# Attention values as rows of tokens: four heads to a job, the weights as the moving side

## The chip, the cores and the metric

The kernel runs on one core of one Trainium2 chip. The metric is the time of one execution on the device in microseconds (us). The kernel before takes 3025.03 us, the median of three runs (3024.79, 3025.03 and 3029.89).

## What is computed

Two transformer blocks follow each other on 256 tokens of width 2048. The change lies in the first one, in its mixer. One projection of the normed input gives queries, keys and values of two attentions of eight heads each, width 128 a head. The first is stick-breaking attention, the second a softmax over keys that an indexer picks; only the second's queries and keys go through rope.

```
proj = h @ w_in
q_a, k_a, v_a, q_b, k_b, v_b, qi, ki, wi, g_a, g_b = split(proj)
y_a = stick_breaking_attention(q_a, k_a, v_a) @ w_a          # 8 heads of 128
y_b = dsa_attention(rope(q_b), rope(k_b), v_b, rope(qi), rope(ki), wi) @ w_b
merged = sigmoid(g_a) * y_a + sigmoid(g_b) * y_b
out = merged @ w_o
```

In both attentions the last step is `w @ v`, a sum over tokens, so it needs the values with tokens on the 128 partitions.

## The kernel before

Every matrix product is a list of *jobs* that one loop, `run`, works off in order. A job of the projection covers 128 output columns. Its weights come in one DMA of 1 MB from `w_in` into a tile `raw` (16 K-tiles of 128x128). The job goes in four *slices* of four K-tiles. For each slice ScalarE (ACT) rounds the weights to fp32r (`whi`) and VectorE (DVE) takes the rest (`wlo`); ACT does so six slices ahead of TensorE (PE), DVE five (`LEAD`). The activations `h` were split in the same way before. TensorE then does three matmuls for each K-tile, `whi·h_hi`, `whi·h_lo` and `wlo·h_hi`, with the 128x128 weights as the stationary side and the 256 tokens as the moving side: 12 matmuls a slice, 48 a job. The result stands in a PSUM tile `g` with output columns on the partitions and tokens along the row.

When a job's last slice has been issued, `run` calls its epilogue `epi`, and then `advance`, as it does after each slice. `advance` lets up to three generators of the list `fill` go one step; each `yield n` of a generator puts its next step off by n slices. What a generator issues on TensorE therefore stands between two slices. An engine takes its instructions in the order in which they were written.

The heads' jobs come as q, k, v of the first head, then of the second, and so on: eight heads of the stick-breaking attention, then eight of the other. The epilogues are:

- `cp_epi` (q and k of the first attention): ACT copies `g` into an SBUF tile `a`.
- `rp_epi` (q and k of the second): four DVE operations, `rope`.
- `v_epi` (values of both): ACT copies `g` to `a`; one slice later a generator transposes the two 128x128 halves on TensorE into a PSUM tile `m` (line 800), and ACT copies them to the tile that the attention reads.

With the value job's epilogue the head's own generator, `sb_gen` or `dsa_gen`, is put into `fill`. It yields until its head's values are there, and then issues the product of queries and keys into an `m` tile as its first step. The later steps (softmax, and `pv`, the product with the values) come up to nine slices later. Beside them run the indexer (`index_gen`, from the first value job on) and a background sum for the modulation on DVE (`acc<-ra,csil,acc`).

All matmuls are issued by the helper on line 271, all ACT operations on line 229, DVE's on lines 242, 256 and 262. In the kernel after, these lines stand one further down.

Of the kernel before, what the change touches and what calls it, by code (L numbers as in the profile page):

```python
# [17 lines left out]
D = 2048  # L18
KT = 16
S = 256  # L20
# [103 lines left out]


class Job:
    def __init__(self, chunks, mv, n, epi, pre=None, outs=None, group=None, need=None, gate=False):
        self.chunks = chunks
        self.mv = mv
        self.n = n  # L130
        self.epi = epi
        self.pre = pre
        self.nk = sum(c[1] for c in chunks)
        self.outs = outs or [(0, self.nk)]
        self.group = group
        self.need = need
        self.gate = gate


class Builder:  # L140
# [258 lines left out]
    def run(self, jobs):  # L399
        order = []  # L400
        i = 0
        while i < len(jobs):
# [5 lines left out]
            for j in grp:  # L408
                sl, k = [], 0
                for ci, (_, nk) in enumerate(j.chunks):  # L410
                    for o in range(0, nk, 4):
                        n = min(4, nk - o)
# [7 lines left out]
        chunks = []  # L420
# [100 lines left out]
        for i, (j, ci, o, k, n) in enumerate(order):  # L521
            if j.gate:
                if (i - gi) % 4 == 0:
                    gated(i)
                continue
            if j.group == "h1":
                j.need(k + n)
                pump_dma()
            if self.lazy:
                pump_hi(i + LEAD)  # L530
                pump_lo(i + LOMIN)
                for x in range(LOMIN + 1, LEAD):
                    if self.backlog() < QW:
                        pump_lo(i + x)
            else:
                pump_lo(i + LEAD - 1)
                pump_hi(i + LEAD)
                pump_lo(i + 1)
            if id(j) not in ps:
                if j.pre is not None:  # L540
                    j.pre()
                ps[id(j)] = [self.pg.tile([128, 512], F32, name="g", tag="g") for _ in j.outs]
            if j.need is not None:
                j.need(min(j.nk, k + n + 4))
            hi, lo = wt.pop(i)
            for q in range(n):
                kk = k + q
                oi = next(x for x, (a0, n0) in enumerate(j.outs) if a0 <= kk < a0 + n0)
                a0, n0 = j.outs[oi]
                out = ps[id(j)][oi][:, :j.n]  # L550
                mh, ml = j.mv(kk)
                self.mm(out, hi[:, q], mh, start=(kk == a0), stop=False)
                self.mm(out, hi[:, q], ml, start=False, stop=False)
                self.mm(out, lo[:, q], mh, start=False, stop=(kk == a0 + n0 - 1))
            if k + n == j.nk:
                j.epi(*ps.pop(id(j)))
            self.advance()
# [230 lines left out]
        self.busy = False  # L788
        yield

    def v_epi(self, store, h):
        def epi(ps):
            t = self.a()
            self.act(t[:, :S], ps[:, :S])

            def g():
                yield
                p = self.mps()
                for k in range(2):
                    self.nc.tensor.transpose(p[:, 128 * k:128 * k + 128], t[:, 128 * k:128 * k + 128], self.ident)  # L800
                o = self.a()
                self.act(o[:, :S], p[:, :S])
                store[h] = o
                yield
            self.later(g())
        return epi

    def sb_gen(self, h):
        scale = 128.0 ** -0.5
        while h not in self.va:  # L810
            yield
        q, k, v = self.qa.pop(h), self.ka.pop(h), self.va.pop(h)
        zp = self.mps()
        self.mm(zp[:, 0:256], k[:, 0:128], q[:, 0:256])
        self.mm(zp[:, 256:384], k[:, 128:256], q[:, 128:256])
        zs = self.sc()
        self.act(zs, zp[:, :384], scale=scale)
        e = self.sc()
        self.act(e, zs, AF.Abs)
        yield 2  # L820
        self.act(e, e, AF.Exp, scale=-1.0)
        self.act(e, e, AF.Ln, bias=1.0)
        sp = self.sc()
        self.stt(sp, zs, 0.0, e, ALU.max, ALU.add)
        past, npast = self.cmm("past"), self.cmm("npast")
        for o in (0, 256):
            self.mul(sp[:, o:o + 128], sp[:, o:o + 128], past)
            self.add(zs[:, o:o + 128], zs[:, o:o + 128], npast)
        yield 4
        cp = self.mps()  # L830
        tri = self.cmm("tri")
        self.mm(cp[:, 0:128], tri, sp[:, 0:128])
        self.mm(cp[:, 128:256], tri, sp[:, 128:256], stop=False)
        self.mm(cp[:, 128:256], self.ones, sp[:, 256:384], start=False)
        self.mm(cp[:, 256:384], tri, sp[:, 256:384])
        self.sub(zs, zs, cp[:, :384])
        self.act(zs, zs, AF.Exp)
        yield 3
        self.pv(zs, v, self.ya, h)
        yield  # L840
# [8 lines left out]

    def dsa_gen(self, h):  # L850
        scale = 128.0 ** -0.5
        while h not in self.vb or self.g_idx in self.fill:
            yield
        q, k, v = self.qb.pop(h), self.kb.pop(h), self.vb.pop(h)
        lp = self.mps()
        self.mm(lp[:, 0:128], q[:, 0:128], k[:, 0:128])
        self.mm(lp[:, 128:384], q[:, 128:256], k[:, 0:256])
        L = self.sc()
        self.stt(L, lp[:, :384], scale, self.smask)
        nm, sm, rs = self.tiny(), self.tiny(), self.tiny()  # L860
        segs = ((0, 128), (128, 384))
        for i, (lo, hi) in enumerate(segs):
            self.nc.vector.tensor_reduce(nm[:, i:i + 1], L[:, lo:hi], mybir.AxisListType.X, ALU.max, negate=True)
        yield 2
        for i, (lo, hi) in enumerate(segs):
            self.act(L[:, lo:hi], L[:, lo:hi], AF.Exp, bias=nm[:, i:i + 1], accum_out=sm[:, i:i + 1])
        self.nc.vector.reciprocal(rs[:, 0:2], sm[:, 0:2])
        for i, (lo, hi) in enumerate(segs):
            self.ts(L[:, lo:hi], L[:, lo:hi], rs[:, i:i + 1])
        yield 3  # L870
        pt = self.mps()
        for o in (0, 128, 256):
            self.nc.tensor.transpose(pt[:, o:o + 128], L[:, o:o + 128], self.ident)
        p = self.sc()
        self.act(p, pt[:, :384])
        yield 2
        self.pv(p, v, self.yb, h)
        yield

    def build_mixer(self):  # L880
# [9 lines left out]
        def wj(epi, pre=None, group=None):  # L890
            jobs.append(Job([(ap["w_in"][nb[0]], KT)], mvh, S, epi, pre, group=group, need=lambda k: self.mod1(k)))
            nb[0] += 1
# [12 lines left out]
        def cp_epi(store, hh):  # L905
            def epi(ps):
                t = self.a()
                self.act(t[:, :S], ps[:, :S])
                store[hh] = t
            return epi  # L910

        def rp_epi(store, hh):
            def epi(ps):
                store[hh] = self.rope(ps, self.cosq, self.sinq)
            return epi
# [3 lines left out]
        def with_gen(epi, make, lst):  # L919
            def f(ps):  # L920
                epi(ps)
                lst.append(self.later(make()))
            return f

        for hh in range(NH):
            wj(cp_epi(self.qa, hh), pre=start_idx if hh == 0 else None)
            wj(cp_epi(self.ka, hh))
            wj(with_gen(self.v_epi(self.va, hh), lambda hh=hh: self.sb_gen(hh), sbg))
        for hh in range(NH):
            wj(rp_epi(self.qb, hh))  # L930
            wj(rp_epi(self.kb, hh))
            wj(with_gen(self.v_epi(self.vb, hh), lambda hh=hh: self.dsa_gen(hh), dsg))

        mg = {}
        self.mg = mg
# [1015 lines left out]


_W = {
    "w_in": (89, 128, KT, 128), "w_ada": (D, 6 * D), "w_a": (KT, 128, 8, 128), "w_b": (KT, 128, 8, 128),
    "w_o": (KT, 128, KT, 128), "w_up": (2 * FT, 128, KT, 128), "w_down": (NQ, KT, 128, FQ, 128),
    "w_in_2": (52, 128, KT, 128), "lora": (8, 128, 4, 128), "w_out_2": (KT, 128, KT, 128),
    "w_gu_2": (2 * FT, 128, KT, 128), "w_down_2": (NQ, KT, 128, FQ, 128),
# [3 lines left out]
def _blocks(w, order=None):  # L1961
    k, n = w.shape
    b = w.reshape(k // 128, 128, n // 128, 128).transpose(2, 1, 0, 3)
    if order is not None:
        b = b[order]
    return np.ascontiguousarray(b)
# [15 lines left out]
def layout(inp):  # L1982
# [13 lines left out]
    qi = w[:, o[6]:o[7]].reshape(D, 8, 2, 2, 32).transpose(0, 1, 3, 2, 4).reshape(D, 1024)  # L1996
    cols = [kw, qi]
    for h in range(NH):
        for s in range(3):
            cols.append(w[:, o[s] + 128 * h:o[s] + 128 * h + 128])  # L2000
    for h in range(NH):
        for s in range(3, 6):
            cols.append(w[:, o[s] + 128 * h:o[s] + 128 * h + 128])
    for s in (9, 10):
        for j in range(KT):
            cols.append(w[:, o[s] + 128 * j:o[s] + 128 * j + 128])
    out["w_in"] = _blocks(np.concatenate(cols, 1))
    out["w_ada"] = np.ascontiguousarray(g["w_ada"][0])
    out["w_a"] = _blocks(g["w_a"][0])
    out["w_b"] = _blocks(g["w_b"][0])  # L2010
# [82 lines left out]
```

## Time and profile before

| what | value |
|---|---|
| median of three runs | 3025.03 us |
| the profiled execution's own time | 3029.85 us |
| its span in the profile | 3028.1 us |
| TensorE busy, share of the span | 98% |
| VectorE busy | 72% |
| ScalarE busy | 52% |
| granted TensorE clock, mean | 0.99 |

The profiled execution is one execution, taken by the hardware profiler; its span is what the trace covers, and its own time is 1.75 us more. It lies at the upper end of the three runs. TensorE's busy share is that of a pipeline, in which a matmul's row begins when the one before it is still on its way; the time between two starts tells the pace.

### The profile page before, as it was taken

The page shows a single profiled execution, that of the slowest core. Times are in us where ns is not written, and L with a number is a line of the kernel's source. Part 1 is how long each engine was busy: PE and PEld are TensorE (multiplying, and loading weights), DVE is VectorE, ACT ScalarE, POOL GpSimd, SP SyncE. Part 2 cuts the span into 40 slices and gives each one's busy share as a digit, 9 for nine tenths or more (in the row PEclk, how much of TensorE's full clock was granted, in tenths as well). Part 3 has the DMA queues.
Part 4 walks back from the last instruction along what each step waited for, and adds up shares of the span by engine and source line. Part 5 has one row for each costly group of instructions (what it writes and reads, how often), then busy time and mean ns, then how long its engine had stood idle before and what let it go on. Part 6 is the DMA issues. An engine that isn't in the chain of part 4 may idle for free.

```text
span 3028.1 us, 66212 instructions
## 1 busy us (share of the span) xinstructions
PE 2975.4 (98%) x27088; PEld 2944.3 (97%) x27088; DVE 2185.2 (72%) x4516; ACT 1573.9 (52%) x3214; POOL 161.6 (5%) x295
## 2 busy tenths in 40 slices
PE   7999999999999999999999999999999999999997
PEld 7999999999999999999999999999999999999997
DVE  6787798677887667676677867777577556566565
ACT  1256544444556556565567545444565555454454
POOL 1000000000210000000002000001000000000002
PEclk9799999999999999999999999999999999999998
DMA  9867677787875554555545433233445454554543
GB/s 343 307 219 250 220 261 264 255 288 263 316 261 184 179 190 168 202 181 177 189 163 188 160 116 116 89 108 125 140 151 197 167 198 173 202 181 167 198 162 129
DMA packets 123473, 594.18 MB, mean 196 GB/s; under 512 B 12832, under 2 KB 19360, under 8 KB 81056
## 3 DMA queue, kind: packets, MB, share of 16 engines
q1 hardware_dynamic: 103200, 518.60, 48.9%
q0 software_dynamic: 19968, 71.35, 7.4%
q8 instruction: 212, 3.47, 0.4%
q14 instruction: 93, 0.76, 0.1%
HBM read 585.68 MB, written 4.21 MB: 195 GB/s over the span
## 4 chain that ended last, share of the span: by engine, by line
PE 95%; DVE 3%; DMA 2%; ACT 0%; issue 0%; SPq 0%; POOL 0%; DVEq 0%; ACTq 0%; POOLq 0%
PE g L271 85%; PE m L271 9%; DMA ch<-w_ada 1%; DVE wlo L242 0%; DMA a<-xT 0%; DVE a L262 0%; DVE a L242 0%; PE m L1414 0%; DVE o L242 0%; DMA cm<-cmask 0%; DVE fa L262 0%; DMA raw<-w_up 0%; ACT a L229 0%; DVE acc L262 0%; DVE p L242 0%
## 5 line engine op out<-in xcount | busy, mean ns | idle before, releaser
L271 PE MATMUL g<-a,whi 128*128 128x256 f32 (+2 forms) x11920 | 2187.2, 285 | 2.4 <-ACT a L229 1.9
L271 PEld LDWEIGHTS g<-a,whi 128*128 128x128 f32 x11920 | 1845.7, 189 | 14.1 <-ACT a L229 2.0
L271 PE MATMUL g<-a,wlo 128*128 128x256 f32 (+3 forms) x5960 | 1684.1, 283 | 1.5 <-DVE wlo L242 1.5
L229 ACT ACTIVATE whi<-raw 128x512 fp32r<-128x512 f32 (+1 forms) x1852 | 1093.4, 617 | 519.3 <-PE g L271 495.5
L242 DVE TENSOR_TENSOR wlo<-raw,whi 128x512 fp32r<-128x512 f32 (+1 forms) x1852 | 1212.9, 681 | 132.2 <-ACT whi L229 130.8
L271 PEld LDWEIGHTS g<-a,wlo 128*128 128x128 f32 x5960 | 1127.1, 189 | 2.9 <-DVE wlo L242 2.6
L271 PE MATMUL g<-h,whi 128*128 128x256 f32 x1408 | 248.9, 281 | 0.0
L271 PE MATMUL g<-ex,whi 128*128 128x258 f32 x1232 | 227.1, 284 | 0.0
L271 PEld LDWEIGHTS g<-h,whi 128*128 128x128 f32 x1408 | 214.9, 188 | 0.0
L271 PE MATMUL g<-h,wlo 128*128 128x256 f32 x704 | 197.8, 281 | 0.0
L271 PEld LDWEIGHTS g<-ex,whi 128*128 128x128 f32 x1232 | 191.3, 190 | 0.0
L262 DVE SCALAR_TENSOR_TENSOR acc<-ra,csil,acc 128x512 f32<-128x512 f32 x240 | 182.1, 759 | 3.9 <-DMA ra<-w_ada 3.9
L229 ACT ACTIVATE a<-a 128x256 f32<-128x256 f32 (+5 forms) x303 | 120.9, 410 | 106.4 <-DVE a L242 79.6
L271 PE MATMUL g<-ex,wlo 128*128 128x258 f32 x616 | 174.9, 284 | 0.3 <-DVE wlo L242 0.3
L262 DVE SCALAR_TENSOR_TENSOR a<-a,pc 128x255 f32<-128x255 f32 (+5 forms) x340 | 163.6, 482 | 5.5 <-ACT a L229 0.5
L229 ACT ACTIVATE a<-a,pc 128x256 f32<-128x256 f32 (+2 forms) x214 | 116.8, 547 | 58.6 <-DVE a L242 53.2
L242 DVE TENSOR_TENSOR a<-g,rb 128x258 f32<-128x258 f32 x80 | 34.1, 426 | 154.4 <-PE g L271 154.4
L635 POOL TENSOR_TENSOR a<-a 128x256 f32<-128x256 f32 x59 | 54.1, 927 | 1673.1 <-ACT a L229 1618.2
L229 ACT ACTIVATE a<-g 128x256 f32<-128x256 f32 (+3 forms) x121 | 46.2, 384 | 179.8 <-PE g L271 179.6
L271 PEld LDWEIGHTS g<-h,wlo 128*128 128x128 f32 x704 | 135.2, 192 | 0.0
L271 PE MATMUL m<-p 64*64 64x64 f32 x3328 | 133.6, 219 | 0.1
L262 DVE SCALAR_TENSOR_TENSOR a<-a 128x256 f32<-128x256 f32 (+3 forms) x275 | 116.6, 424 | 11.7 <-ACT a L229 7.7
(171 smaller groups left out, 1848.3 us busy)
## 6 DMA issues: line engine op xcount, KB each, us to landing
raw<-w_in SPq DMA_DIRECT2D x141, 1024.0 KB, 5.8
raw<-w_up SPq DMA_DIRECT2D x88, 1024.0 KB, 4.9
raw<-w_down SPq DMA_DIRECT2D x128, 704.0 KB, 4.1
raw<-w_gu SPq DMA_DIRECT2D x88, 1024.0 KB, 4.9
ra<-w_ada POOLq DMA_DIRECT2D x128, 512.0 KB, 5.4
ch<-w_ada SPq DMA_DIRECT2D x64, 512.0 KB, 7.5
raw<-w_o SPq DMA_DIRECT2D x16, 1024.0 KB, 7.2
raw<-w_out SPq DMA_DIRECT2D x32, 512.0 KB, 3.6
```

Source lines behind the costliest of these rows:

```text
L229: self.nc.scalar.activation(out, in_, f, **kw)
L242: self.nc.vector.tensor_tensor(out, a, b, op)
L262: self.nc.vector.scalar_tensor_tensor(out, a, s, b, op0, op1)
L271: self.nc.tensor.matmul(out, l, r, start=start, stop=stop)
L635: self.nc.gpsimd.tensor_tensor(q[:, :n], q[:, :n], acc[:, :n], ALU.add)
```

## The change

The values are no longer 16 jobs of 128 columns but four *wide* jobs of 512 columns, four heads each. The weights of the values leave `w_in` for an array `w_v`, in which a slice is one K-tile of 512 columns. In a wide job the activations are the stationary side, 128 tokens at a time, and the weights are the moving side, 512 columns: per slice two token halves by three matmuls, each into one of two PSUM tiles. The result has tokens on the partitions, so `v_epi` copies 128x128 pieces, eight ACT operations for four heads, and the transposes and the copies behind them go. A wide job stands ahead of each group of four heads, whose jobs are then q and k alone. The heads' generators are now put into `fill` by the epilogue of k, and wait for k instead of v.

```diff
@@ run
-            for q in range(n):
+            if j.wide:
+                kk, last = k // 4, k + n == j.nk
+                wh, wl = (t.rearrange("p q c -> p (q c)") for t in (hi, lo))
+                mh, ml = j.mv(kk)
+                for t in range(2):
+                    out, c = ps[id(j)][t], slice(128 * t, 128 * t + 128)
+                    self.mm(out, mh[:, c], wh, start=kk == 0, stop=False)
+                    self.mm(out, mh[:, c], wl, start=False, stop=False)
+                    self.mm(out, ml[:, c], wh, start=False, stop=last)
+            for q in range(0 if j.wide else n):
@@ v_epi
-    def v_epi(self, store, h):
-        def epi(ps):
-            t = self.a()
-            self.act(t[:, :S], ps[:, :S])
-
-            def g():
-                yield
-                p = self.mps()
-                for k in range(2):
-                    self.nc.tensor.transpose(p[:, 128 * k:128 * k + 128], t[:, 128 * k:128 * k + 128], self.ident)
-                o = self.a()
-                self.act(o[:, :S], p[:, :S])
-                store[h] = o
-                yield
-            self.later(g())
+    def v_epi(self, store, h0):
+        def epi(*ps):
+            for h in range(4):
+                o = store[h0 + h] = self.a()
+                for t in range(2):
+                    self.act(o[:, 128 * t:128 * t + 128], ps[t][:, 128 * h:128 * h + 128])
         return epi
@@ sb_gen
-        while h not in self.va:
+        while h not in self.ka:
@@ dsa_gen
-        while h not in self.vb or self.g_idx in self.fill:
+        while h not in self.kb or self.g_idx in self.fill:
@@ build_mixer
+        def vj(s, h0, pre=None):
+            w = ap["w_v"][2 * s + h0 // 4]
+            jobs.append(Job([(w[g], KT) for g in range(4)], mvh, S, self.v_epi(self.vb if s else self.va, h0), pre,
+                            outs=[(0, 2 * KT), (2 * KT, 2 * KT)], wide=True))
+
         for hh in range(NH):
-            wj(cp_epi(self.qa, hh), pre=start_idx if hh == 0 else None)
-            wj(cp_epi(self.ka, hh))
-            wj(with_gen(self.v_epi(self.va, hh), lambda hh=hh: self.sb_gen(hh), sbg))
+            if hh % 4 == 0:
+                vj(0, hh, pre=start_idx if hh == 0 else None)
+            wj(cp_epi(self.qa, hh))
+            wj(with_gen(cp_epi(self.ka, hh), lambda hh=hh: self.sb_gen(hh), sbg))
         for hh in range(NH):
+            if hh % 4 == 0:
+                vj(1, hh)
             wj(rp_epi(self.qb, hh))
-            wj(rp_epi(self.kb, hh))
-            wj(with_gen(self.v_epi(self.vb, hh), lambda hh=hh: self.dsa_gen(hh), dsg))
+            wj(with_gen(rp_epi(self.kb, hh), lambda hh=hh: self.dsa_gen(hh), dsg))
```

**Where the product of queries and keys stands on TensorE, stick-breaking attention, second head.** Before, one slice into the next head's q job (`g_2201`): the two transposes of the values (`a_2192`), then the product of k (`a_2103`) and q (`a_2006`), whose jobs had ended four and eight slices ahead of the value job's end.

```order
L271 MATMUL g_2201<-a_419,whi_2089 128x256
L271 MATMUL g_2201<-a_414,wlo_2108 128x256
L800 MATMUL m_2217<-cm_88,a_2192 128x128 [waits Activation_49]
L800 MATMUL m_2217<-cm_88,a_2192 128x128
L271 MATMUL m_2222<-a_2006,a_2103 128x256 [waits PE_49]
L271 MATMUL m_2222<-a_2006,a_2103 128x128
L271 MATMUL g_2201<-a_576,whi_2110 128x256
```

After, between the last matmul of that head's own k job (`g_2168`) and the first of the next q job (`g_2263`); k is `a_2247`, which ACT copies from `g_2168`.

```order
L272 MATMUL g_2168<-a_924,whi_2124 128x256
L272 MATMUL g_2168<-a_919,wlo_2141 128x256
L272 MATMUL m_2252<-a_2159,a_2247 128x256 [waits Activation_49]
L272 MATMUL m_2252<-a_2159,a_2247 128x128
L272 MATMUL g_2263<-a_398,whi_2145 128x256
```

The product moved from five slices behind the end of its k job to directly behind it, and the transposes are gone.

**The same place in the second attention, second head.** Before, the k operand is `a_4200`, the q operand `a_4114`.

```order
L271 MATMUL g_4296<-a_414,wlo_4213 128x256
L800 MATMUL m_4309<-cm_88,a_4287 128x128 [waits Activation_49]
L800 MATMUL m_4309<-cm_88,a_4287 128x128
L271 MATMUL m_4314<-a_4200,a_4114 128x128 [waits PE_49]
L271 MATMUL m_4314<-a_4200,a_4114 128x256
L271 MATMUL g_4296<-a_576,whi_4215 128x256
```

After, k is `a_4106`, which rope makes from `g_4023`, the PSUM tile of the job that ends in the row above the product.

```order
L272 MATMUL g_4023<-a_924,whi_3977 128x256
L272 MATMUL g_4023<-a_919,wlo_3991 128x256
L272 MATMUL m_4111<-a_4106,a_4011 128x128 [waits DVE_49,PE_49]
L272 MATMUL m_4111<-a_4106,a_4011 128x256
L272 MATMUL g_4125<-a_398,whi_3995 128x256
```

Here too the product now stands at the end of the k job itself, and its wait is one for DVE.

**The same head's rope on VectorE.** Before: the last operation of k's rope (`a_4200`), then nine other operations, then the first one that reads the product (`m_4314`).

```order
L242 TENSOR_TENSOR a_4200<-a_4198,a_4199 128x256 [waits DVE_49]
L242 TENSOR_TENSOR a_4210<-m_4205,a_4209 128x256 [waits Activation_49]
L242 TENSOR_TENSOR wlo_4213<-raw_3906,whi_4184 128x512 [waits DMAHW4_49]
L256 TENSOR_SCALAR acc_4230<-ra_4231,csil_93 128x512 [waits DMASW0_49]
L242 TENSOR_TENSOR wlo_4236<-raw_3906,whi_4215 128x512 [waits Activation_49]
L256 TENSOR_SCALAR acc_4230<-ra_4231,csil_93 128x512
L242 TENSOR_TENSOR wlo_4253<-raw_3906,whi_4238 128x512 [waits Activation_49]
L242 TENSOR_TENSOR wlo_4269<-raw_3906,whi_4255 128x512 [waits PE_49,Activation_49]
L256 TENSOR_SCALAR acc_4230<-ra_4233,csil_93 128x512 [waits DMASW1_49]
L242 TENSOR_TENSOR wlo_4292<-raw_3989,whi_4273 128x512 [waits DMAHW5_49,PE_49,Activation_49]
L262 SCALAR_TENSOR_TENSOR sc_4317<-m_4314,smask_942 128x384 [waits PE_49]
```

After: a split of the head before (`a_4083`) and one of the weights, the rope of k (`a_4106`), and behind it at once the operation that reads the product (`m_4111`).

```order
L243 TENSOR_TENSOR a_4083<-m_4078,a_4082 128x256 [waits Activation_49]
L243 TENSOR_TENSOR wlo_4086<-raw_3740,whi_4061 128x512
L243 TENSOR_TENSOR a_4105<-g_4023,a_449 64x256 [waits PE_49]
L243 TENSOR_TENSOR a_4105<-g_4023,a_449 64x256
L243 TENSOR_TENSOR a_4104<-g_4023,a_344 128x256
L243 TENSOR_TENSOR a_4106<-a_4104,a_4105 128x256 [waits DVE_49]
L263 SCALAR_TENSOR_TENSOR sc_4114<-m_4111,smask_942 128x384 [waits PE_49]
```

What lay between rope and the reader of the product is gone; both now follow each other with the product itself between them on TensorE.

## Rows read from the trace of the kernel before

**Rows 1.** The page: busy time by engine, and the chain that ended last.

```profile
PE 2975.4 (98%) x27088; PEld 2944.3 (97%) x27088; DVE 2185.2 (72%) x4516; ACT 1573.9 (52%) x3214; POOL 161.6 (5%) x295
...
PE 95%; DVE 3%; DMA 2%; ACT 0%; issue 0%; SPq 0%; POOL 0%; DVEq 0%; ACTq 0%; POOLq 0%
```

**Rows 2.** Waits of TensorE, 120 to 560 us: us in total, times, longest.

```profile
PE m L739 <- ACT a L229: 2.0, 1, 2.0
PE m L271 <- ACT sc L229: 1.5, 1, 1.5
```

**Rows 3.** Timeline, transposes of a head: start us, us, engine, line, operation, count.

```profile
492.36 0.38 PE L800 MATMUL m<-cm,a 128*128 128x128 f32 x2
...
492.58 0.39 PE L271 MATMUL m<-a 128*128 128x128 f32 x2
```

**Rows 4.** Timeline, TensorE alone, 99 matmuls of 256 columns: first and last.

```profile
644.97 0.28 PE L271 MATMUL g<-a,wlo 128*128 128x256 f32 x1
...
656.65 0.29 PE L271 MATMUL g<-a,wlo 128*128 128x256 f32 x1
```

**Rows 5.** Timeline, TensorE alone, 90 matmuls of 272 columns: first and last.

```profile
1660.93 0.29 PE L271 MATMUL g<-a,wlo 128*128 128x272 f32 x1
...
1672.22 0.28 PE L271 MATMUL g<-a,wlo 128*128 128x272 f32 x1
```

**Rows 6.** Timeline at half the clock: three matmuls of 256 columns, then the next.

```profile
2242.97 0.63 PE L271 MATMUL g<-a,whi 128*128 128x256 f32 x2
...
2243.39 0.41 PE L271 MATMUL g<-a,wlo 128*128 128x256 f32 x1
...
2243.61 0.42 PE L271 MATMUL g<-a,whi 128*128 128x258 f32 x1
```

**Rows 7.** Timeline, end of a value job: last matmul, ACT's copy of its result.

```profile
218.89 0.28 PE L271 MATMUL g<-a,wlo 128*128 128x256 f32 x1
...
219.21 0.38 ACT L229 ACTIVATE a<-g 128x256 f32<-128x256 f32 x1 [0.73 <-PE g L271]
```

**Rows 8.** Timeline, a product with the values that waits for ACT.

```profile
214.81 0.52 ACT L229 ACTIVATE sc<-sc 128x384 f32<-128x384 f32 x1 [4.17 <-DVE sc L242]
...
215.39 0.94 PE L271 MATMUL m<-sc,a 128*128 128x128 f32 x6 [1.48 <-ACT sc L229]
...
216.08 0.36 PE L271 MATMUL g<-a,whi 128*128 128x256 f32 x1
```

**Rows 9.** Timeline, end of a k job of the second attention, rope behind it.

```profile
371.15 0.28 PE L271 MATMUL g<-a,wlo 128*128 128x256 f32 x1
371.27 0.83 PE L271 MATMUL m<-sc,a 128*128 128x128 f32 x6
371.47 1.29 DVE L242 TENSOR_TENSOR a<-g,a 64x256 f32<-64x256 f32 x3 [1.08 <-PE g L271]
371.86 0.48 PE L271 MATMUL g<-a,whi 128*128 128x256 f32 x2
...
372.80 0.42 DVE L242 TENSOR_TENSOR a<-a 128x256 f32<-128x256 f32 x1
```

**Rows 10.** Timeline, the next head's k job: last matmul, first operation of rope.

```profile
408.94 0.28 PE L271 MATMUL g<-a,wlo 128*128 128x256 f32 x1
...
409.55 0.43 DVE L242 TENSOR_TENSOR a<-g,a 64x256 f32<-64x256 f32 x1
```

**Rows 11.** Timeline, a k job of the first attention: last matmul, ACT's copy.

```profile
251.46 0.28 PE L271 MATMUL g<-a,wlo 128*128 128x256 f32 x1
...
252.69 0.37 ACT L229 ACTIVATE a<-g 128x256 f32<-128x256 f32 x1
```

**Rows 12.** Stretches: busy us and counts of PE, PEld, DVE, ACT, POOL; PEclk; DMA share; GB/s.

```profile
135.00:142.00 7.00, 4.97 (x42) 4.74 (x42) 6.38 (x17) 3.75 (x8) 0.00 (x0) 1.00 0.23 92
397.93:473.46 75.53, 75.53 (x639) 75.32 (x638) 69.31 (x136) 36.85 (x80) 6.86 (x13) 1.00 0.76 261
2230.00:2242.00 12.00, 6.59 (x47) 6.22 (x46) 6.99 (x24) 5.69 (x13) 0.00 (x0) 0.78 0.06 26
2243.00:2246.00 3.00, 3.00 (x16) 3.00 (x16) 2.93 (x8) 1.64 (x4) 0.00 (x0) 0.50 0.01 3
```

More of the change, by code (lines that the diff above doesn't have):

```diff
@@ L126, with __init__ @@
 class Job:
-    def __init__(self, chunks, mv, n, epi, pre=None, outs=None, group=None, need=None, gate=False):
+    def __init__(self, chunks, mv, n, epi, pre=None, outs=None, group=None, need=None, gate=False, wide=False):
         self.chunks = chunks
@@ L137, in __init__ @@
         self.gate = gate
+        self.wide = wide
 class Builder:
@@ L1953 @@
 _W = {
-    "w_in": (89, 128, KT, 128), "w_ada": (D, 6 * D), "w_a": (KT, 128, 8, 128), "w_b": (KT, 128, 8, 128),
+    "w_in": (73, 128, KT, 128), "w_v": (4, 4, 128, KT, 128), "w_ada": (D, 6 * D), "w_a": (KT, 128, 8, 128), "w_b": (KT, 128, 8, 128),
     "w_o": (KT, 128, KT, 128), "w_up": (2 * FT, 128, KT, 128), "w_down": (NQ, KT, 128, FQ, 128),
@@ L1998, in layout @@
     for h in range(NH):
-        for s in range(3):
+        for s in range(2):
             cols.append(w[:, o[s] + 128 * h:o[s] + 128 * h + 128])
     for h in range(NH):
-        for s in range(3, 6):
+        for s in range(3, 5):
             cols.append(w[:, o[s] + 128 * h:o[s] + 128 * h + 128])
@@ L2007, in layout @@
     out["w_in"] = _blocks(np.concatenate(cols, 1))
+    vs = np.stack([w[:, o[s] + 512 * i:o[s] + 512 * i + 512] for s in (2, 5) for i in range(2)], 0)
+    out["w_v"] = np.ascontiguousarray(vs.reshape(4, 4, 4, 128, 512).transpose(0, 1, 3, 2, 4)).reshape(4, 4, 128, KT, 128)
     out["w_ada"] = np.ascontiguousarray(g["w_ada"][0])
```

## Prediction

> **What bounds the kernel now.** I read the page first. TensorE is busy for 98% of the span, and 95% of the chain that ended last is its own [rows 1]. So a microsecond added to or taken from TensorE's row in the mixer is one of the whole time, unless TensorE waits there anyway. The list of waits says that it hardly does: from 120 to 560 us, which holds all the heads' jobs, there are two, of 2.0 and 1.5 us [rows 2]. The first lies ahead of the value jobs and stays as it is. The stretches show who would be late next: over four heads of the second attention DVE is busy for 69.3 of 75.5 us, ACT for 36.9 [rows 12]. The order of the instructions then tells which of the new waits stand on TensorE's path, and the timeline what each takes.
>
> **What goes: the transposes.** A head's two transposes start at 492.36 and the next product at 492.58, so they hold TensorE for 0.22 us [rows 3]; they stand in a block of such products that stays, so nothing else goes with them. Sixteen heads make 3.5 us. That part I count in full.
>
> **What changes its form: 768 matmuls of 256 columns become 384 of 512.** The columns are as many as before, so the gain is what a matmul costs beside its columns. No row shows 512 columns in fp32r. 99 matmuls of 256 columns take from 644.97 to 656.65, 118.0 ns each [rows 4]; 90 of 272 take from 1660.93 to 1672.22, 125.4 ns each [rows 5]. The 16 columns more cost 7.4 ns, 0.46 a column, and 256 times 0.46 is 118: by these two rows a matmul costs nothing beside its columns, and 512 take 236 ns. The other end comes from the half clock. There three matmuls of 256 columns take 0.64 us, 213 ns each [rows 6], in a stretch whose granted clock was 0.50, the last of [rows 12]; that is 1.2 GHz, and twice the clock would make it 106.7. If the 11.3 ns that are missing at full clock are a fixed cost, half of the matmuls save 384 times 11.3 ns, 4.4 us. But a fixed cost would be seen at the half clock too, unless it hides there, and 256 against 272 leaves no room for it. I take 0, and keep 4.4 us for the range.
>
> The Trainium skill, TensorE: Matmul & The Clock Gate, Back-to-back issue gap, gives the gap between matmuls as the columns over 2.4 GHz plus 2.5 ns. For 256 columns that is 109 ns, and the rows have 118, so the trace does not agree. By the page 512 columns would take 216 ns, and the sum below would be 7.8 us lower.
>
> **What is added: a wait at the end of every k job.** Before, the product of queries and keys stood five slices behind its k job, since the generator waited for the values. Now k's epilogue puts the generator into the list, and its first step comes at once. TensorE has the product directly behind the job's last matmul, and it needs what ACT or DVE still has to make of that job's result. Behind it on TensorE stands the next job, so nothing covers this.
>
> *First attention, ACT's copy.* The end of a value job shows the same step: last matmul at 218.89, copy from 219.21, 0.38 long, so ready at 219.59 [rows 7]. How TensorE takes up work after such a wait is seen once: ACT ends at 214.81 + 0.52 = 215.33, the matmul starts at 215.39, which is 0.05 us behind it (0.06 in rounded rows), and its six products take until 216.08, 0.69 us [rows 8], against 0.59 for the same six without a wait (371.27 to 371.86) [rows 9], so 0.10 more. Without a wait the product would start 0.12 behind the last matmul (371.15 to 371.27) [rows 9]. A head costs 0.32 + 0.38 + 0.05 + 0.10 − 0.12 = 0.73 us, eight heads 5.8.
>
> *Second attention, rope on DVE.* The last matmul of a k job starts at 371.15; rope starts at 371.47, and its last operation ends at 372.80 + 0.42 = 373.22 [rows 9]. A head costs 2.07 + 0.05 + 0.10 − 0.12 = 2.10 us, eight heads 16.8.
>
> Both can be dearer. ACT's copy of a k came 1.23 us behind the last matmul where the head before had ACT in its exponentials [rows 11], 0.91 later than above: at most 7.3 us over eight heads. By the yields of `sb_gen` the last exponential came six slices behind the product, so one slice ahead of the next k copy; now that the product comes a slice sooner, it is two slices ahead, so I take the short delay. Rope began 0.61 behind the last matmul where DVE still had a split to do [rows 10], 0.29 later: at most 2.3 us over eight. DVE's work for a head now falls into 8 slices instead of 12, which speaks for lateness; but each wait of TensorE gives DVE 2 us to catch up, so I take 0 here as well.
>
> **What is hidden.** The values' 32 copies (one ahead of the transposes, one behind, for 16 heads) become 32 of half the size, eight behind each wide job; ACT idles for half of the second attention's stretch [rows 12], and the next slices' `whi` stand six slices ahead. If that cover were gone, a burst of eight at less than 0.38 us each [rows 7] would be 3 us four times. The weights' loads are the same 1 MB pieces, in another order on SP's queue. DVE's operations are the same. The wait of 1.5 us in the first head's product with the values [rows 8] may go or stay, as the indexer's work now meets that head at another point; I leave it, and keep it for the range.
>
> **The sum.** −3.5 + 0 + 5.8 + 16.8 = +19.1 us. On the profiled execution's own time, 3029.85, that is 3048.9 (a span of 3047.2). This execution lies 4.8 us above the median of the runs; on the median, 3025.03, it is 3044.1, and that I predict. The bounds: 4.4 and 1.5 us less give 3038.2; 7.3 and 2.3 us more give 3053.7.
>
> **Rivals.** *The wide matmuls run at the bare pace of their columns.* Twice 118.0 less twice 106.7 is 22.7 ns, times 384 is 8.7 us, and the time 3035.4. The half clock speaks for it [rows 6], the 272 columns against it [rows 5]. This is where the page's rule, with its 2.5 ns, would lead; by its own row at 256 columns the trace does not bear it out.
>
> *Not slower: TensorE goes on past the wait.* If the product can stand aside while the next job's matmuls, whose operands are ready, run, the 22.6 us are gone and 3.5 stay as gain: 3021.5, which no measurement tells from no change. Against it: such matmuls stood behind the product that waited in [rows 8], and TensorE idled for 1.48 us. It decides if the sixteen waits together cost less than about 9.5 us, 0.6 a head.
>
> *The clock falls.* Eight pauses of 2 us may take the granted clock down. Once it fell, in 2230 to 2242 us, where TensorE was busy for 6.6 of 12 us and the mean was 0.78 [rows 12]: 0.22 × 12 / 0.5 = 5 us of it at half, and 4 more up to 2246, so 4.6 us lost at least. Eight of these are 37 us, and the time 3081. Against it: from 135 to 142 TensorE paused for the 2.0 us of [rows 2], was busy for 5.0 of 7, and the clock stayed at 1.00; the waits here come 12 us or more apart.
>
> **How the numbers follow.** I give 0.71 to the sum as it stands with its bounds, 0.17 to the bare pace, 0.06 to the falling clock, 0.04 to no wait, and leave 0.02. The range goes from the bare pace, 3035, to the dear waits, 3054, and 2 us on, since executions of this kernel differ by up to 5 us. What a measurement can tell from no change is about 0.2%, 6 us. Slower by more than that: 0.94; within it: 0.04; faster: 0.02.
>
> **What the profile after would show.** The list of waits has eight of TensorE on DVE's rope, 0.32 + 1.75 + 0.05 − 0.28 = 1.84 us each (it counts from the end of the matmul before, 0.28 behind its start), and eight on ACT's copy, 0.47 each; 14.7 and 3.8 us in all, between 190 and 560 us. Matmuls of 512 columns start 236 ns apart; 225 would show the fixed cost, 213 the bare pace. The transposes and 384 matmuls are gone. The granted clock stays at 1.00 there. I would be wrong if the waits are missing or far shorter, or if a new wait of TensorE on `wlo` or `whi` shows that DVE or ACT can't follow in the denser heads.

## The result, and the profile after

The changed kernel takes 3046.39 us (median of 4 runs, 3045.66 to 3047.99), the kernel before 3025.56 beside it (4 runs, 3024.79 to 3029.89). The ratio is 1.0067 (95% interval 1.0055 to 1.0079): slower, 2.3 us above the forecast and inside its range. The profiled execution took 3046.24 us with a span of 3044.5. Of the experiments below, one execution of f2_before_two (4096.54 us, mean granted clock 0.66) and one of f3_after_spare (4224.03 us, 0.64) lie far above all others and stand in no median and no ratio.

The page of the changed kernel: busy time by engine, shares of the chain that ended last, and the costliest group of the last stage (busy us, mean ns of one, idle).

```profile
PE 2969.8 (98%) x26672; PEld 2918.8 (96%) x26672; DVE 2186.6 (72%) x4516; ACT 1576.5 (52%) x3214; POOL 162.8 (5%) x295
...
PE 93%; DVE 4%; DMA 1%; ACT 1%; issue 1%; SPq 0%; DVEq 0%; ACTq 0%
...
L272 PE MATMUL g<-h,whi 128*128 128x256 f32 x1408 | 239.7, 276 | 0.0
```

Against [rows 1], TensorE has 416 matmuls fewer and 5.6 us less to do, and the chain is its own for 93% instead of 95%: the kernel is longer with less work, so it waits. The list of TensorE's waits in the changed kernel, from 120 to 600 us (us in total, times, longest), says for what:

```profile
PE m L272 <- DVE a L243: 16.3, 8, 2.5
PE m L272 <- ACT a L230: 6.2, 8, 2.8
PE m L749 <- ACT a L230: 2.0, 1, 2.0
```

Where [rows 2] had a wait of 1.5 us of a product with the values, there are now eight waits on rope and eight on ACT's copy of k. The third row is the old wait ahead of the value jobs.

The timeline of the changed kernel around one wait on rope (start us, us, engine, line, operation, count, and in brackets the idle time before and its releaser):

```profile
395.51 0.28 PE L272 MATMUL g<-a,wlo 128*128 128x256 f32 x1
...
395.89 1.30 DVE L243 TENSOR_TENSOR a<-g,a 64x256 f32<-64x256 f32 x3
...
397.22 0.42 DVE L243 TENSOR_TENSOR a<-a 128x256 f32<-128x256 f32 x1
...
397.79 1.31 PE L272 MATMUL m<-a 128*128 128x128 f32 x4 [2.00 <-DVE a L243]
```

The chain is that of [rows 9], now with TensorE behind it: last matmul of the k job at 395.51, rope to 397.64, the product of queries and keys at 397.79. The wait of 2.00 us is 0.16 longer than forecast, and rope begins 0.38 instead of 0.32 behind the matmul.

The stretches of the changed kernel from one such product to the next (busy us and counts of PE, PEld, DVE, ACT, POOL; granted clock; DMA share; GB/s) show what the forecast had only as a rival:

```profile
382.55:397.79 15.24, 13.24 (x110) 13.01 (x110) 13.05 (x28) 6.26 (x14) 1.06 (x2) 1.00 0.64 209
397.79:414.56 16.77, 14.77 (x110) 14.41 (x110) 13.21 (x28) 6.37 (x14) 1.06 (x2) 0.90 0.55 184
398.12:401.53 3.41, 3.41 (x17) 3.22 (x16) 2.36 (x6) 0.99 (x4) 0.00 (x0) 0.50 0.57 226
```

Both heads have 110 matmuls and a wait of 2 us. In the second the granted clock was 0.50, that is 1.2 GHz, from 398.12 to 401.53, just behind the wait, and the head is 1.53 us longer. That happened behind five of the eight waits on rope: 7.7 us.

**Where the difference arises.** Three matmuls mark the same points of the work in both traces: the first on `ex` (FFN1's, behind the whole mixer), the first on `h` of the last stage and the last on `h`. First the timeline of the kernel before, profiled once more (b_again below), from the old wait of 2.0 us on:

```profile
139.24 0.29 PE L739 MATMUL m<-cm,a 16*128 16x16 f32 x2 [2.03 <-ACT a L229]
...
863.33 0.40 PE L271 MATMUL g<-ex,whi 128*128 128x258 f32 x2
...
2390.43 0.40 PE L271 MATMUL g<-h,whi 128*128 128x256 f32 x2
...
3007.74 0.28 PE L271 MATMUL g<-h,wlo 128*128 128x256 f32 x1
```

and that of the changed kernel:

```profile
140.06 0.29 PE L749 MATMUL m<-cm,a 16*128 16x16 f32 x2 [2.03 <-ACT a L230]
...
890.81 0.40 PE L272 MATMUL g<-ex,whi 128*128 128x258 f32 x2
...
2415.84 0.43 PE L272 MATMUL g<-h,whi 128*128 128x256 f32 x2
...
3024.30 0.28 PE L272 MATMUL g<-h,wlo 128*128 128x256 f32 x1
```

The first stretch, with all heads, went from 724.09 to 750.75 us, +26.7. The second lost 2.1, about what two profiles of one kernel differ by there (1525.0 and 1526.7). The last, whose instructions the change doesn't touch, went from 617.31 to 608.46, −8.9. So the mixer pays more than the forecast 19.1 us, and a third of it comes back in a stage that nobody edited. The experiments had both to explain.

### The profile page after: what moved, and what is told of

It is laid out like the page before. It is cut to its first block, busy times and chain, and to the rows that moved or that the text cites. A ratio compares the mean times of both kernels' runs of the same rounds, so it can differ in the third digit from the quotient of the medians.

```text
span 3044.5 us, 65404 instructions
## 1 busy us (share of the span) xinstructions
PE 2969.8 (98%) x26672; PEld 2918.8 (96%) x26672; DVE 2186.6 (72%) x4516; ACT 1576.5 (52%) x3214; POOL 162.8 (5%) x295
## 4 chain that ended last, share of the span: by engine, by line
PE 93%; DVE 4%; DMA 1%; ACT 1%; issue 1%; SPq 0%; DVEq 0%; ACTq 0%
PE g L272 84%; PE m L272 8%; DMA ch<-w_ada 1%; DVE a L243 1%; DVE wlo L243 1%; DVE fa L263 1%; DVE a L263 1%; ACT a L230 0%; PE m L1422 0%; DVE o L243 0%; DMA cm<-cmask 0%; ACT whi L230 0%; SPq L1796 0%; ACT sc L230 0%; DVE p L243 0%
## 5 line engine op out<-in xcount | busy, mean ns | idle before, releaser
L272 PE MATMUL g<-a,whi 128*128 128x256 f32 (+3 forms) x11408 | 2095.9, 285 | 3.0 <-ACT a L230 2.3
L272 PEld LDWEIGHTS g<-a,whi 128*128 128x128 f32 x11408 | 1769.7, 190 | 14.4 <-ACT a L230 2.4
L272 PE MATMUL g<-a,wlo 128*128 128x256 f32 (+3 forms) x5704 | 1613.9, 283 | 0.9 <-DVE wlo L243 0.9
L272 PEld LDWEIGHTS g<-a,wlo 128*128 128x128 f32 x5704 | 1082.8, 190 | 1.8 <-DVE wlo L243 1.8
L272 PE MATMUL g<-h,whi 128*128 128x256 f32 x1408 | 239.7, 276 | 0.0
L230 ACT ACTIVATE a<-g 128x256 f32<-128x256 f32 (+4 forms) x137 | 46.6, 365 | 169.5 <-PE g L272 169.2
```

What stands on the lines that cost most here:

```text
L230: self.nc.scalar.activation(out, in_, f, **kw)
L272: self.nc.tensor.matmul(out, l, r, start=start, stop=stop)
```

## The experiments

The table holds what was measured: the median, the ratio to the kernel before on the same chip, TensorE's listed waits on ACT and on DVE (rope) between 140 and 600 us, the half-clock stretches in the first of the three stretches, and the same three stretches in us, read from each profile.

| run | us (runs) | ratio (95%) | ACT, rope us | half clock | first | second | last |
|---|---|---|---|---|---|---|---|
| b_again | 3029.71 (1) | | 1.5, 0 | 0 | 724.1 | 1527.1 | 617.3 |
| changed kernel | 3046.39 (4) | 1.0067 (1.0055–1.0079) | 6.2, 16.3 | 5 | 750.8 | 1525.0 | 608.5 |
| a_again | 3044.69 (5) | 1.0064 (1.0052–1.0077) | 6.2, 16.3 | 6 | 752.3 | 1526.7 | 608.5 |
| e5_gen_at_k | 3053.91 (4) | 1.0084 (1.0070–1.0098) | 3.3, 16.7 | 4 | 752.1 | 1526.4 | 616.4 |
| e4_filled | 3035.62 (6) | 1.0033 (1.0022–1.0045) | 6.2, 0.4 | 1 | 744.6 | 1525.6 | 608.5 |
| e2_late_dsa | 3032.39 (11) | 1.0015 (1.0007–1.0024) | 6.2, 0.5 | 1 | 727.5 | 1527.1 | 618.6 |
| e1_late | 3025.53 (11) | 0.9996 (0.9987–1.0005) | 2.3, 0.5 | 1 | 721.8 | 1527.3 | 618.6 |
| e6_sb3 | 3023.63 (11) | 0.9993 (0.9984–1.0002) | 0, 0.6 | 0 | 718.4 | 1528.3 | 618.6 |
| e3_two_heads | 3012.97 (5) | 0.9958 (0.9944–0.9971) | 2.2, 0 | 0 | 721.5 | 1525.5 | 607.9 |
| f1_before_spare | 3024.81 (11) | 0.9993 (0.9984–1.0002) | 1.5, 0 | 0 | 724.1 | 1526.4 | 615.0 |
| f2_before_two | 3026.30 (10) | 0.9997 (0.9988–1.0006) | 1.5, 0 | 0 | 724.1 | 1528.3 | 617.3 |
| f3_after_spare | 3045.06 (4) | 1.0058 (1.0044–1.0071) | 6.2, 16.3 | 6 | 752.3 | 1529.5 | 608.4 |
| f4_sb3_spare | 3021.17 (11) | 0.9983 (0.9974–0.9992) | 0, 0.5 | 0 | 718.3 | 1527.0 | 616.2 |

In e2_late_dsa, e1_late and f3_after_spare one half-clock stretch came behind the old wait of 2.0 us ahead of the value jobs. In e2_late_dsa that wait ends at 135.68, and the stretch is this:

```profile
136.19:139.60 3.41, 3.41 (x18) 3.41 (x18) 3.27 (x10) 2.18 (x5) 0.00 (x0) 0.50 0.00 0
```

The other eleven profiles have the same wait and a granted clock of 1.00 behind it. From the end of that wait to the product of the first head it is 77.8 us in f3 and 76.3 in the changed kernel, so this stretch costs 1.5 us too, and with it f3 has six in its first stretch, like a_again, and the same 752.3 us.

**b_again**, the kernel before once more.

> The kernel before once more, unchanged, for a second profile. In the one shown, the 704 + 1408 matmuls of the last stage that read h started 118 ns apart; in the profile of the changed kernel the same instructions started 114 ns apart. If that pace belongs to the execution, it may be 114 here, with a time some 8 us lower than the first profile's 3029.85; if it belongs to the kernel, it is 118 again.

Its first stretch is 0.5 us from that of the profile shown ahead of the prediction (724.6), and its last one equal (617.3), so the slower pace of the last stage came again: a stretch of one kernel repeats to a microsecond or two, better than the whole time does.

**e5_gen_at_k: the waits alone.** The kernel before, with the generators put into the list by k's epilogue; value jobs and transposes stay.

```
-        while h not in self.va:
+        while h not in self.ka:
...
-            wj(cp_epi(self.ka, hh))
-            wj(with_gen(self.v_epi(self.va, hh), lambda hh=hh: self.sb_gen(hh), sbg))
+            wj(with_gen(cp_epi(self.ka, hh), lambda hh=hh: self.sb_gen(hh), sbg))
+            wj(self.v_epi(self.va, hh))
```

(and the same for `dsa_gen`, with the values taken out of their store at the product that needs them.)

> The kernel before, values in jobs of their own with transposes, and only the generators put into the list by k's epilogue, as in the changed kernel (the values are fetched later, at their product). The theory: the sixteen waits are there without any wide job, 6 us on ACT's copy and 18 us on rope, so 3048 to 3052 us, and up to 8 us more if the clock falls as well. The rival of denser heads: no head is denser than before, so 3025 us.

```profile
PE m L271 <- DVE a L242: 16.7, 8, 2.5
PE m L271 <- ACT a L229: 3.3, 7, 0.5
PE m L739 <- ACT a L229: 2.0, 1, 2.0
```

The list has fifteen of the changed kernel's sixteen waits, without any of its value jobs, and the first stretch is as long (752.1). The slowdown is the generator's place. The time, 3053.91, lies above the forecast sum, and four half-clock stretches of some 1.5 us came too.

**e2_late_dsa and e1_late: the changed kernel with the products put off.** e2 puts off the second attention's by two slices, e1 also the first attention's by one.

```
+        yield 1
         q, k, v = self.qa.pop(h), self.ka.pop(h), self.va.pop(h)
...
+        yield 2
         q, k, v = self.qb.pop(h), self.kb.pop(h), self.vb.pop(h)
```

> The changed kernel, with the product put off by two slices in the second attention alone. The theory: the eight waits on rope (16.3 us in the list of waits) and the falls of the clock go, the eight on ACT's copy stay with some 8 us: 3027 to 3030 us. If the clock fell for another reason than the waits on rope, it still falls five times and the time is 3034 or more. The rival of denser heads: above 3035.

> The changed kernel, with the product of queries and keys put off: by one slice in the first attention, by two in the second. The theory (the sixteen waits at the end of the k jobs, and the falls of the clock behind them, are the whole loss): no waits of TensorE on the copy of k or on rope, a granted clock of 1.00 through the heads, and what the change gains alone, so 3019 to 3022 us against 3025.6 before. The rival (the heads' steps now fall into 8 slices instead of 12, so DVE and ACT are late wherever the product stands): waits of TensorE come back at other rows, and the time stays above 3030.

e2's first stretch is 23.3 us shorter than the changed kernel's. The parts make 23.6: 15.8 of listed waits on rope, 1.6 for the restart behind the six that went (0.26 each by the forecast's sum) and 6.2 for the clock, since four half-clock stretches fewer came. None is left behind a wait on rope; one came behind the old wait. With e1 another 5.7 go, and the slowdown is gone. The rival, that denser heads are themselves dearer, falls. But e1 missed its own number by 3.5 us and e2 by 2.4. In both the last stage is 1.3 us longer than in the kernel before, which their edits do not explain; the larger part of e1's miss is in its list:

```profile
PE m L272 <- ACT a L230: 2.3, 1, 2.3
PE m L749 <- ACT a L230: 2.0, 1, 2.0
PE m L272 <- DVE a L243: 0.5, 2, 0.3
```

One head still waits 2.3 us, and it is the one that waits 2.8 in the changed kernel. There the timeline shows what holds ACT's copy up:

```profile
229.21 0.28 PE L272 MATMUL g<-a,wlo 128*128 128x256 f32 x1
...
229.50 0.41 DVE L791 MATCH_REPLACE8 smask<-ty,smask 128x256 f32<-128x256 f32 x1
229.82 0.55 DVE L243 TENSOR_TENSOR sc<-sc,m 128x384 f32<-128x384 f32 x1
...
230.40 0.52 ACT L230 ACTIVATE sc<-sc 128x384 f32<-128x384 f32 x1 [3.67 <-DVE sc L243]
230.83 1.14 ACT L230 ACTIVATE whi<-raw 128x512 fp32r<-128x512 f32 x2
231.87 0.36 ACT L230 ACTIVATE a<-g 128x256 f32<-128x256 f32 x1
...
232.28 0.48 PE L272 MATMUL m<-a 128*128 128x256 f32 x1 [2.80 <-ACT a L230]
```

The last matmul of the k job starts at 229.21. ACT stands idle for 3.67 us in front of head 0's exponential, which waits for a subtraction on DVE; DVE is in the indexer's top-k there. Queued behind it on ACT are two `whi` and head 1's copy, which starts 2.66 us behind the matmul instead of the 0.31 of a quiet head. That is the late copy that the forecast kept for its upper bound, at one head of eight, and there 2.3 us late instead of 0.9.

**e6_sb3: the same with three slices in the first attention** (`yield 3` for `yield 1`).

> The kernel with the later start of the heads (e1_late), with the SB heads put off by three slices instead of one. e1_late still has one wait of 2.3 us, of head 1's first product on ACT's copy of k; two slices more are 24 matmuls of 118 ns, 2.8 us, so that wait should go: 2.3 us less than e1_late, about 3023, and no wait of TensorE on ACT's copies between 200 and 360 us. Rival (the products put off delay the heads' own chain, or fill less): no change from e1_late, 3025.5 +-1.

```profile
PE m L749 <- ACT a L230: 2.0, 1, 2.0
PE m L272 <- DVE a L243: 0.6, 2, 0.3
```

No wait on a copy is left, and the first stretch is 3.5 us shorter than e1's, 1.5 of it because this profile has no half-clock stretch behind the old wait. It is 5.7 shorter than before: that is what the projection into rows is worth there by itself. The interval of its time still touches 1.

**e4_filled: the waits on rope filled with work.** In the changed kernel TensorE gets 17 matmuls that nobody reads where it waits for rope.

```
+        fp = self.mps()
+        fh = self.h[0][0]
+        for i in range(17):
+            self.mm(fp[:, :S], fh[:, 0:128], fh)
```

> The changed kernel with 17 added fp32r matmuls of 256 columns ahead of each DSA head's first product (their result is read by nobody), so that TensorE works where it waited for rope. 17 x 118 ns are 2.0 us, as long as the wait, so the time spent there stays; what can go is the short half-clock stretch behind five of the eight rope waits, 3.4 us each, worth 16.77 - 15.24 = 1.54 us a head or 7.7 us in all. Theory (the falls follow from the idle TensorE and cost what they seem to): no half-clock stretch between 380 and 540 us, and 7.7 us less than the changed kernel, about 3038 to 3040. Rival (a fall costs nothing or comes anyway): 3046 +-2.

The stretch of e4_filled that holds eight heads:

```profile
374.00:518.00 144.00, 143.59 (x1102) 137.89 (x1101) 121.66 (x244) 61.16 (x136) 12.19 (x23) 1.00 0.67 220
```

TensorE is busy and the clock stays at 1.00. Nothing of the heads' own work came sooner, yet the first stretch is 6.2 us shorter than the changed kernel's with five half-clock stretches and 7.7 shorter than a_again's with six; e4_filled has one, at the end of a wait of 2.8 us in the first attention. Four and five fewer at 1.54 us are 6.2 and 7.7. So it was the idle TensorE that cost the clock, and this is its price. The time itself, 3035.62, is 2.4 us below the forecast and 9.1 below a_again's; the stretches do not account for that, and the six executions lie 9 us apart (3031.92 to 3041.14).

**a_again: is the faster last stage the execution's or the kernel's?**

> The changed kernel once more, unchanged, to see whether the 114.0 ns at which the matmuls of the last stage followed one another in its profile (118.0 in the kernel before, and in all four others so far) stays with the kernel or with the execution. If with the kernel: 114 again, and 3046 +-2. If with the execution: 118 in this profile, and a span some 8.5 us longer, near 3054.

The kernel's: 608.5 again, and the median within 2 us.

**e3_two_heads: 256 moving columns instead of 512.** e1_late with jobs of two heads, so 768 narrower matmuls.

```
...
-            for h in range(4):
+            for h in range(2):
...
-            w = ap["w_v"][2 * s + h0 // 4]
+            w = ap["w_v"][4 * s + h0 // 2]
...
```

> The kernel with the later start of the heads (e1_late) with jobs of two heads: 256 moving columns instead of 512, 768 matmuls instead of 384. Theory (a matmul of 256 columns follows another in 118 ns, one of 512 in 232.5): 3.5 ns a pair more, 384 x 3.5 ns = 1.3 us longer than e1_late, beyond that only what two-head jobs move in the order; 3025 to 3030. Rival of the bare pace (213 ns for 512, a fixed cost for each matmul of 11 ns): the 512-column matmuls would be worth 4 us more, 3030 to 3034.

The timeline of the changed kernel, 52 steps of 512 columns, first and last:

```profile
444.62 0.39 PE L272 MATMUL g<-wlo,a 128*128 128x512 f32 x1
...
456.64 0.39 PE L272 MATMUL g<-whi,a 128*128 128x512 f32 x1
```

and that of e3_two_heads, 59 steps of 256:

```profile
338.36 0.36 PE L272 MATMUL g<-whi,a 128*128 128x256 f32 x1
...
345.41 0.28 PE L272 MATMUL g<-whi,a 128*128 128x256 f32 x1
```

12.02 / 52 is 231.2 ns, 7.05 / 59 is 119.5; by these two windows the wide form saves 384 × (239.0 − 231.2) = 3.0 us. They are not quite typical. Over all steps of the value jobs at clock 1.00 with nothing else between them (200 to 265 and 100 to 140 ns), the means are 232.0 ns in seven traces of the wide form and 118.2 in e3, so 384 × (236.4 − 232.0) = 1.7 us. The first stretches, 721.8 and 721.5, agree once it is said what else differs: e1's holds the half-clock stretch behind the old wait, 1.5 us, and two short waits on rope, 1.0 with their restarts, and e3's neither; without these e3's is 2.2 longer. Both theories missed the time: at 3012.97 it is the fastest of all, and 10.6 of its 12.6 us on e1_late lie in the last stage (607.9 against 618.6), not in the value jobs.

**f1 to f4: what sets the pace of the last stage?** Its 2112 matmuls on `h` stand in four unbroken runs of 528, with other jobs between them. In the traces they follow one another in 117.8 ns in some kernels and in 113.4 in others. A first theory read a rule out of TensorE's instruction count.

```
+        r = self.force(hid, q * FQ + k)
+        if (q, j, k) == (0, 0, 0):
+            p = self.mps()
+            for _ in range(1):
+                self.nc.tensor.matmul(p[:, :S], r[0][:, 0:128], r[0], start=True, stop=True)
...
```

f1 is this edit in the kernel before, f2 the same with `range(2)`, f3 the edit of f1 in the changed kernel and f4 in e6_sb3.

> The kernel before with one spare fp32r matmul of 256 columns (two instructions, weight load and matmul; its result is read by nobody) just ahead of the last stage's first matmul on h, nothing else. In the seven programs run so far, the count of TensorE's instructions in the trace ahead of that matmul is 43921 (before), 43929, 43085 (twice, e1_late and e2_late_dsa) and 43090 where these 2112 matmuls follow one another in 117.8 ns, and 43087 (changed kernel), 43856 and 43360 where they do in 113.4: remainders by four of 1, 1, 1, 1, 2 against 3, 0, 0. Theory (the position in the instruction stream sets that pace): 43923 has remainder 3, so 113.4 ns, 2112 x 4.4 ns = 9.2 us less, about 3017 (3015 to 3019). Rival (something else that goes with the changed kernel's order): 117.8 ns and no change, 3026 +-1.5.

> The same with two spare matmuls (four instructions): remainder 1 as in the kernel before. Theory of the position by four: 117.8 ns and the time of the kernel before, 3026 +-1.5. Rival (any spare instruction there changes the pace): 113.4 ns and 3017.

> The changed kernel with one spare matmul at the same place: 43087 + 2 has remainder 1. Theory of the position: 117.8 ns, 2112 x 4.4 = 9.2 us more than the changed kernel, about 3054 (3051 to 3056); this would be what the change costs with the last stage as it was before. Rival (the pace belongs to the changed kernel): 113.4 ns and 3045 +-1.5.

> The kernel with the heads' first products put off by three and two slices (e6_sb3, 43090 instructions ahead) with one spare matmul at the same place: remainder 0. Theory: 113.4 ns and 9.2 us less than e6_sb3, about 3014 (3012 to 3017). Rival: 117.8 ns and 3023.5 +-1.5.

The theory falls: f3 keeps its pace though the remainder changed, and f1 and f4 gain about 2 us and not 9 (f1's interval touches 1; its last stretch shows the gain). The groups of f1_before_spare show what happened, in its first run (2386 to 2448 us) and then in its second (2573 to 2635):

```profile
L271 PE MATMUL g<-h,whi 128*128 128x256 f32 x352 | 59.9, 276 | 0.0
...
L271 PE MATMUL g<-h,whi 128*128 128x256 f32 x350 | 61.9, 281 | 0.0
```

The run right behind the spare matmul has the short matmuls, 276 ns as in the changed kernel; the other three have 281 as before. f4 shows the same, and 528 × 4.4 ns = 2.3 us is what both gained in the last stretch (2.4 and 2.3). Two spares (f2) change nothing. So a run settles within its first 48 matmuls on one of two paces and keeps it to the end, and one spare matmul ahead can change which, as in f1 and f4; it need not, as f3 shows. Why one run gets 113.4 and another 117.8 stays open: the steps ahead of the runs differ from kernel to kernel, and I found no rule in them that holds for all.

## Why the prediction was right, and where its sum was not

**The place and the kind of the waits: right.** Eight on rope and eight on ACT's copy, where the program's order put them; e5 makes the slowdown with fifteen of them and no wide job, e1 removes it. That the product can stand aside is refuted.

**The size of the waits: too small.** Forecast as listed, 14.7 and 3.8 us; measured 16.3 and 6.2. Rope's were 1.91 to 2.00 us in seven heads and 2.45 in one. Seven of ACT's were 0.47 to 0.53, as forecast, and one 2.80: the late copy of the upper bound came true once, through ACT's queue. With the 0.26 that the forecast added to each for the restart, sixteen waits cost 26.7 instead of 22.6.

**The transposes: right.** 416 matmuls fewer, and e6's first stretch 5.7 us below b_again's, of which 3.5 are the transposes by the forecast's price, 1.6 the wait of 1.5 us that went, 1.8 the wide form, less 1.1 for the two short waits on rope that e6 still has.

**The wide form: between the two ends, near the one taken.** 231.2 ns in the window shown and 232.0 in the mean, against 236 forecast, 225 for a fixed cost and 213 for the bare pace: 1.8 us gained by the window, 1.5 by the mean, where the sum had 0; 1.8 is counted here. By the formula in the Trainium skill, TensorE: Matmul & The Clock Gate, Back-to-back issue gap, it would be 216 ns. The section says, as the forecast does not, that this formula is for an isolated matmul, and gives about 131 ns for 512 columns in a sustained stream; the trace agrees with neither.

**The clock: the step that failed.** It was a rival with 0.06 and had no place in the sum, because a wait of 2.0 us at 140 us left the clock at 1.00. That was one pause in one profile: behind the same wait the clock fell in three of the fourteen. In the changed kernel it fell behind five waits on rope, and each fall cost 1.54 us, not the 4.6 taken from the fall that began at 2236.6 us in the kernel before, which lasted 10.2 us, three times as long. "The granted clock stays at 1.00 there" was wrong.

**What the sum had not at all:** the last stage's −8.9 us.

With these the first stretch comes to 26.7 − 1.6 − 3.5 − 1.8 + 7.7 = 27.5 us, and 26.7 were measured; the 0.8 that is over is not settled. With the last stage −8.9 and the second −2.1 that is 15.7, and the start of the program, 0.8 later here, makes 16.5 of the 16.6 by which the spans of these two profiles differ. On the medians the difference is 20.8, since b_again, like the execution shown ahead of the prediction, lay above its median. So the forecast's +19.1 came within 2 us of the result because what it had left out or mis-sized nearly cancels: 7.7 for the clock and 4.1 for the waits on one side, 1.8 for the wide form, 1.6 for the wait that went and 8.9 for the last stage on the other. Its direction and its mechanism are shown; its closeness is not its merit.

## What to carry to other kernels

When a consumer is moved up to its producer, price the full latency of the engine between them, once for each time that it is waited for, and look at what stands in that engine's queue in the one busy place, not only in the quiet one. Two or three slices of other work between producer and consumer (e6_sb3) gave the whole loss back. A pause that left the clock alone in one trace is no rule for the next: the old wait of 2.0 us brought a fall in three profiles of fourteen. And compare traces stage by stage at fixed points of the work: a total that fits can be the sum of two errors, and the fastest kernel here (e3_two_heads) owes most of its gain to a stage that its edit does not touch.

## What the hardware did that I had not expected

A long run of equal matmuls has two steady paces at the same granted clock of 1.00, 113.4 and 117.8 ns for 256 columns; it keeps one of them over 528 matmuls, has the same in both profiles of the kernel before and in both of the changed kernel, and one spare matmul ahead of the run can change it. Over the last stage that is 9 us, more than most edits of this study.

A pause of about 2 us (1.91 to 2.52) lowered the granted clock to 0.50 behind four to six of eight waits on rope (five and six in the two profiles of the changed kernel, five in f3_after_spare, four in e5_gen_at_k), for 3.41 us each time, and it did so in the middle of an otherwise full TensorE. The falls at the waits filled in e4_filled did not come. Which of the eight it is behind was not the same in every kernel, and none of the changed kernel's waits on ACT's copies, 2.80 us among them, had one, though the same wait of 2.8 us in e4_filled did.
